# Spectrum stores on GpSimd's queue, a new layout of the attention's inputs, a bias table in DRAM and query parts in two runs, in a one-core encoder kernel

## The chip, the cores and the metric

The kernel runs on one core of a Trainium2 chip, as one program in one launch. The metric is the device time of an execution in microseconds (us). A core has TensorE (PE in the profile, with its weight loads under PEld), VectorE (DVE), ScalarE (ACT), GpSimd (POOL) and SyncE (SP). Each runs its own instruction stream in order, semaphores join the streams, and any of SP, ACT and POOL can issue DMAs from its stream; such an issue stands in the engine's order like any other instruction.

## The reference

One layer of an encoder on 2048 + 256 = 2304 tokens of width 1024, in fp32:

```python
h = rmsnorm(x); q, k, v, u, qm = split(h @ w_in)           # 8 + 2 + 2 heads of 64, 256 channels, 4 heads
y_attn = window attention of q on k, v (|t-s| <= 128, bias -2^-(head+1) * |t-s|, sink logit per head)
y_four = real(fft2(u)) over (positions, channels of a group)
y_mem  = cross attention of qm on k, v of 256 memory tokens
x = x + concat(rmsnorm(y_attn), rmsnorm(y_four), rmsnorm(y_mem)) @ w_out
x = x + square(relu(rmsnorm(x) @ w_ff1)) @ w_ff2
return rmsnorm(x)
```

## The kernel before, in words

**Arithmetic.** An fp32 product is done as three matmuls of a split: `hi` is a copy of a number in the matmul's rounded fp32 type, `lo` the rest. `hi_of` (L103) makes the first on ScalarE, `lo_of` (L106) the second on VectorE. `scaled_split` (L169, L170) does both with a gain, for the output weights: `woh` on ScalarE, then `wol` on VectorE, which needs `woh`. All matmuls go through one helper, L100. `rstd_of` (L133, L134) makes 1/root of a mean square on GpSimd.

**Stages.** First the in-projection. Its groups g = 0 to 8 hold 256 tokens each, with two memory groups between; a group's tokens are normalised, transposed, split and multiplied by the resident `win`. Each group stores k, v and q to DRAM scratch (`Kd`, `Vd`, `Qd`). A part of q is copied from the PSUM tile `pj` in eight pieces of 64 partitions: four by ScalarE (L420, the rounded copy) and four by VectorE (L421, the rest), each VectorE piece after the ScalarE piece that it subtracts. In groups 2 to 6 a side job, `w2_sums`, loads tiles of the second feed-forward weight, subtracts parts of them on GpSimd and stores them to DRAM, through two buffers `big`. In groups 7 and 8 another side job, `fourier`, does the DFT over positions: it combines channels into `X` and `fbig` (L530 on GpSimd among others), loads the DFT matrices `seq` from GpSimd's queue (L445), multiplies (`po`), and `spread` turns a result into rows: copies L482 and L484, squaring L491 (`fjk`), rstd on GpSimd, scaling L493 (`fst`), and a store of 128 KB to `Yd0`, `Yd1` or `Zd` (L495, from ScalarE's queue). `mirror` (L473) copies rows of `Zd` to `Yd0`, in reversed order, in two DMAs, also from ScalarE's queue. The last group's three q stores (L424) go from ScalarE's queue too; those of the groups before go from SyncE's.

Then the attention with the out-projection. Blocks of 128 tokens are loaded in pairs (`load_pair`): keys `kb` (L621) and values `vb` (L634) of up to four blocks, queries `qb` of each block (L632), memory keys and values `km`, `vm` (L646, L648). For the first pair there is also the table of distances `dist` (L624), from which GpSimd makes the table `bias`, eight heads of 128x384 bf16 (L626). Scores `s` are matmuls of `qb` and `kb`; `p` (L661, VectorE) adds the bias and takes the least, L664 (ScalarE) is the exponential; `t` transposes it for the product with `vb`. Fourier rows `y` come back from DRAM (L758). `open_out` loads the eight 128x1024 slices `wos_0` to `wos_7` of the output weights (L813) into three buffers and splits them; the out-projection `op` of a block needs all eight pairs of `woh` and `wol`, and the block's `x` again (`xr`, L825). The feed-forward stage, with its own tilings, takes the rest of the time, from about 870 us on; the change does not touch it.

**What sets the order.** The program text gives what depends on what; a scheduler puts the instructions of each engine in order when the program is built, and that order is fixed. Pools of tiles lie on a left and a right side of the on-chip memory (SBUF). A later pool may lie over an earlier one; each of its tiles then waits for the last users of the tiles beneath it. The attention's pools lie over the in-projection's `fpool` (left): before the change `kb_0` over `wl0`, `vb_0` over the tiles of x, `bias` and `qb_0` over `X` and neighbours, `qb_1`, `km`, `vm` over the small Fourier buffers and `fbig0`, and the buffers of `p`, one of which held `dist`, over `fbig0` and `fbig1`. The output weights (right side) lie over `win`.

Of the kernel before, what the change touches and what calls it, by code (L numbers as in the profile page):

```python
# [12 lines left out]
F32R = mybir.dt.float32r  # L13
BF16 = mybir.dt.bfloat16
AF = mybir.ActivationFunctionType
ALU = mybir.AluOpType
# [4 lines left out]
P = 128  # L21
# [72 lines left out]
def trunk(ctx, tc, x, mem, w_in, w_mem, w_out, w1, w2, gains, g_final, sinks, ident_d, dist_d, cdft_d, seq_d, y):  # L94
# [20 lines left out]
    mhalf = cpool.tile([P, 4], F32, name="mhalf")  # L115
    dve.memset(mhalf, -0.5)

    Qd = dpool.tile([NBLK, P, NQ, P], F32R, name="Qd")
    Kd = dpool.tile([P, 2, 2, T], F32R, name="Kd")
    Vd = dpool.tile([NBLK, P, 2, 2, HD], F32R, name="Vd")  # L120
# [25 lines left out]
    if True:  # L146
# [62 lines left out]
        def w2_sums():  # L209
            ts = {}  # L210
            for j in range(NF // 2 + 1):
                if j < NF // 2:
                    ts[j] = big(f"w2r_{j}")
                    sp.dma_start(ts[j].rearrange("p (k n) c -> p k (n c)", k=2), w2[2 * j:2 * j + 2].rearrange("k p n -> p k n"))
                yield
                if j > 0:
                    b = ts.pop(j - 1)
                    for o, u, v in ((0, 1, 0), (1, 3, 1), (3, 3, 0), (2, 3, 2)):
                        pool.tensor_tensor(out=b[:, o], in0=b[:, u], in1=b[:, v], op=ALU.subtract)
                    pool.dma_start(W2T[j - 1], b)  # L220
                yield

        w2_work = w2_sums()

# [147 lines left out]
        def group(g, side=None):  # L372
# [5 lines left out]
            for mp in (3, 2, 0, 1, 4):  # L378
# [33 lines left out]
                else:  # L412
# [2 lines left out]
                    pv = ps.rearrange("p j (b t) -> p j b t", b=2)  # L415
                    for e in range(2):
                        a = slice(e * HD, (e + 1) * HD)
                        o = slice((1 - e) * HD, (2 - e) * HD)
                        for j in range(2):
                            act.activation(qv[a, e, j], pv[a, j], AF.Copy, scale=-0.125)  # L420
                            dve.scalar_tensor_tensor(out=qv[o, e, j], in0=pv[a, j], scalar=-0.125,  # L421
                                                     in1=qv[a, e, j].bitcast(F32), op0=ALU.mult, op1=ALU.subtract)
                    h0 = {0: 0, 1: 4, 4: 8}[mp]
                    (act if g == 8 else sp).dma_start(  # L424
                        Qd[2 * g:2 * g + 2, :, h0:h0 + 4].rearrange("b p h t -> p b (h t)").bitcast(F32),
                        q.rearrange("p b j e t -> p b (j e t)").bitcast(F32))
                if 2 <= g < 7:
# [38 lines left out]
        def place(ti, r):  # L466
            if ti > 8:
                return Y1[:, ti - 9]
            return Zd[7 - ti] if r else Y0[:, ti]

        def mirror(a):

            act.dma_start(Y0.rearrange("t r c -> r t c")[9 + a:16:2, ::-1], Zd[a:7:2])  # L473


        def spread(ti, po, full):
# [15 lines left out]
            rstd_of(st, 256)  # L492
            act.activation(yr[:, 0:n], yr[:, 0:n], AF.Copy, scale=st)  # L493
            for r in range(n):
                act.dma_start(place(ti, r), yr[:, r])  # L495

        def fourier():
            yield
# [85 lines left out]
        for i, name in enumerate(order):  # L584
            g = int(name[1:])
            if name[0] == "m":
                mem_kv(g, i)
            elif g < 7:
                if g == 3:
                    fe, fab, ffg = f8("fe"), f8("fab"), f8("ffg")  # L590
                group(g)
        for _ in w2_work:
            pass
        side = fourier()
        group(7, side)
        group(8, side)
# [4 lines left out]
    right.close()  # L601
    left.close()
    if True:
        ip = {k: region(left, "left", "in_" + k) for k in ('kk', 'vv', 'bias', 'q', 'mem', 'p')}
        op = region(right, "right", "outproj")
        ps_p = region(right, "right", "ps_p", 1, PSUM)
        inner, banks_ = ExitStack(), ExitStack()
# [6 lines left out]
        def load_pair(b0):  # L614
            r = b0 >= NB0
            first = b0 in (0, NB0)
            last = b0 + 2 in (NB0, NBLK)
            ka, kz = b0 - (not first), b0 + 2 + (not last)
            nk = kz - ka
            kk = ip["kk"].tile([P, 2, 2, 4 * P], F32R, tag="kk", bufs=2, name=f"kb_{b0}")  # L620
            sp.dma_start(kk[:, :, :, 0:nk * P].bitcast(F32), Kd[:, :, :, ka * P:kz * P].bitcast(F32))  # L621
            if b0 == 0:
                dist = ip["p"].tile([P, 1024], BF16, tag="p", bufs=4, name="dist")[:, 0:3 * P]
                sp.dma_start(dist, dist_d)  # L624
                for u in range(NH):
                    pool.tensor_scalar(out=bias[:, u], in0=dist, scalar1=2.0 ** -(u + 1), scalar2=0.0,  # L626
                                       op0=ALU.mult, op1=ALU.add)
            vv = ip["vv"].tile([P, 4, 2, 2, HD], F32R, tag="vv", bufs=2, name=f"vb_{b0}")
            pair = []
            for b in (b0, b0 + 1):  # L630
                q = ip["q"].tile([P, NQ, P], F32R, tag="q", bufs=3, name=f"qb_{b}")
                sp.dma_start(q.bitcast(F32), Qd[b].bitcast(F32))  # L632
                if b == b0:
                    sp.dma_start(vv[:, 0:nk].rearrange("p b v l d -> p b (v l d)").bitcast(F32),  # L634
                                 Vd[ka:kz].rearrange("b p v l d -> p b (v l d)").bitcast(F32))
                lo = max(b - 1, ka)
                hi = min(b + 2, kz)
                stt = bp.tile([P, 40], F32, tag="stats", bufs=4, name=f"stats_{b}")
                pair.append(dict(b=b, r=r, j0=lo - ka, nk=hi - lo, c0=(lo - b + 1) * P, q=q, k=kk, v=vv, st=stt))
            return pair  # L640
# [743 lines left out]
```

## Time and profile before

| | us |
|---|---|
| median of 3 runs (lowest to highest) | 2340.67 (2337.38 to 2342.37) |
| the profiled execution | 2344.84 |
| its span in the trace | 2343.0 |
| TensorE busy in the span | 2229.2 (95%) |
| VectorE, ScalarE, GpSimd busy | 1561.4, 1003.4, 1139.7 |
| last matmul of the in-projection ends | 357.6 |
| first score matmul of the attention | 371.69 |
| first out-projection matmul `op` | 416.70 |

A name in the trace leaves out the number of a buffer (`kb`, `qb`); L621 is line 621 of the kernel. A row of waits says which engine and line waited, for what, how many us in all, how often, and the longest. `<-` after an idle time names what ended it. "issue" is time in which an engine waited for nothing that the profile shows. In a row of DMA issues the last number is the median us from issue to landing.

### The profile page before, as it was taken

To read this page: it belongs to the slowest core of one execution; us is meant where nothing else is said; L and a number is where in the kernel's file an instruction comes from. 1 tells how busy PE (TensorE), PEld (TensorE's weight loads), DVE (VectorE), ACT (ScalarE), POOL (GpSimd) and SP (SyncE) were. 2 spreads that over 40 slices of the span, in tenths; PEclk is the share of its full clock that TensorE was granted. 3 is DMA by queue.
4 is the path that set the end of the run, shared out by engine and by line. 5 is a ranking of instruction groups with operands and counts; after the bars stand their busy time and mean duration, and the time that the engine had idled before them with its cause. 6 is when DMAs were issued, how large, how long until landed. Compare 5 with 4: busy or idle time off the path is not lost.

```text
span 2343.0 us, 35879 instructions
## 1 busy us (share of the span) xinstructions
PE 2229.2 (95%) x12464; PEld 2005.2 (86%) x12464; DVE 1561.4 (67%) x2781; ACT 1003.4 (43%) x2353; POOL 1139.7 (49%) x1023
## 2 busy tenths in 40 slices
PE   7999996999999999999999899999999999999996
PEld 6999995887788878999999788999998889999984
DVE  7333476777677767888888986555557765555567
ACT  6333356766566654444444433222224342222224
POOL 3554031113123035777777685444444765444476
PEclk9999998999999999999999999999999999999998
DMA  8886347445444368766666887555557675555543
GB/s 298 309 296 246 100 136 280 138 148 158 149 145 156 132 238 298 252 222 228 222 229 222 311 262 272 192 191 190 190 191 268 196 258 187 190 189 190 190 163 99
DMA packets 207116, 488.05 MB, mean 208 GB/s; under 512 B 19799, under 2 KB 63319, under 8 KB 204631
## 3 DMA queue, kind: packets, MB, share of 16 engines
q1 hardware_dynamic: 192896, 446.86, 56.2%
q0 software_dynamic: 6848, 29.24, 3.6%
q10 hardware_dynamic: 7191, 9.65, 1.2%
q8 instruction: 99, 1.62, 0.3%
q14 instruction: 82, 0.67, 0.1%
HBM read 341.76 MB, written 144.83 MB: 208 GB/s over the span
## 4 chain that ended last, share of the span: by engine, by line
PE 67%; DVE 8%; DMA 4%; ACT 2%; issue 2%; POOL 1%; SPq 0%; POOLq 0%; ACTq 0%; DVEq 0%
PE y L100 26%; PE op L100 8%; PE pc L100 8%; PE pb L100 8%; PE pa L100 8%; PE pd L100 4%; DMA X2d<-xr 1%; DVE acc L323 1%; PE s L100 1%; PE ot L100 1%; PE t L687 1%; DVE p L661 1%; DMA XTl<-Xn 1%; DVE al L106 1%; PE otm L100 1%
## 5 line engine op out<-in xcount | busy, mean ns | idle before, releaser
L106 POOL TENSOR_TENSOR w2l<-w,w2h 128x512 fp32r<-128x512 f32 x336 | 484.3, 1443 | 494.8 <-ACT w2h L103 490.2
L100 PE MATMUL y<-w2l,ah 128*128 128x512 f32 x966 | 380.9, 395 | 6.4 <-POOL w2l L106 6.4
L100 PE MATMUL y<-w2h,al 128*128 128x512 f32 x966 | 381.9, 396 | 0.0
L100 PE MATMUL y<-w2h,ah 128*128 128x512 f32 x966 | 360.7, 398 | 17.6 <-DVE acc L323 9.0
L103 ACT ACTIVATE ah<-m 128x384 fp32r<-128x384 f32 x240 | 125.8, 524 | 509.5 <-PE y L100 488.0
L106 DVE TENSOR_TENSOR al<-m,ah 128x384 fp32r<-128x384 f32 x240 | 182.9, 763 | 180.2 <-ACT ah L103 167.6
L323 DVE TENSOR_TENSOR acc<-acc,y 128x512 f32<-128x512 f32 x378 | 244.3, 680 | 24.1 <-PE y L100 20.0
L100 PEld LDWEIGHTS y<-w2h,ah 128*128 128x128 f32 x966 | 183.3, 190 | 45.2 <-DVE acc L323 12.1
L100 PE MATMUL pc<-XTh,w1s 128*128 128x384 f32 x768 | 218.8, 340 | 0.8 <-DVE m L323 0.3
L100 PE MATMUL pa<-XTh,w1s 128*128 128x384 f32 x768 | 215.7, 337 | 0.7 <-ACT w1s L103 0.5
L100 PE MATMUL pb<-XTh,w1s 128*128 128x384 f32 x768 | 214.5, 336 | 0.7 <-ACT m L1095 0.7
L103 ACT ACTIVATE w2h<-w 128x512 fp32r<-128x512 f32 x336 | 207.3, 617 | 10.9 <-DMA w1s<-W1D 4.5
L100 PEld LDWEIGHTS y<-w2h,al 128*128 128x128 f32 x966 | 183.3, 190 | 33.1
L100 PEld LDWEIGHTS y<-w2l,ah 128*128 128x128 f32 x966 | 183.3, 190 | 30.4 <-POOL w2l L106 7.8
L100 PE MATMUL pj<-hl_x,winh 128*128 128x256 f32 x720 | 206.1, 288 | 0.7 <-DVE hl_x L106 0.7
L100 PE MATMUL pj<-hh_x,winh 128*128 128x256 f32 x720 | 203.5, 288 | 1.3 <-ACT hh_x L103 1.3
L100 PE MATMUL pj<-hh_x,winl 128*128 128x256 f32 x720 | 204.5, 286 | 0.0
L1068 DVE SCALAR_TENSOR_TENSOR m<-m 128x384 f32<-128x384 f32 x192 | 159.0, 828 | 42.5 <-ACT m L1095 39.0
L100 PEld LDWEIGHTS pc<-XTh,w1s 128*128 128x128 f32 x768 | 142.9, 190 | 10.4 <-DVE m L323 1.4
L100 PEld LDWEIGHTS pb<-XTh,w1s 128*128 128x128 f32 x768 | 141.2, 188 | 8.9 <-ACT m L1095 1.0
L100 PEld LDWEIGHTS pa<-XTh,w1s 128*128 128x128 f32 x768 | 141.6, 188 | 8.3 <-ACT w1s L103 0.8
L100 PEld LDWEIGHTS pj<-hl_x,winh 128*128 128x128 f32 x720 | 139.3, 194 | 1.3 <-DVE hl_x L106 1.2
(243 smaller groups left out, 5181.4 us busy)
## 6 DMA issues: line engine op xcount, KB each, us to landing
w1s<-W1D SPq DMA_DIRECT2D x224, 512.0 KB, 3.5
W1D<-w1s SPq DMA_DIRECT2D x112, 512.0 KB, 3.6
w<-in_w_dram SPq DMA_DIRECT2D x208, 256.0 KB, 3.8
w<-W2T SPq DMA_DIRECT2D x192, 256.0 KB, 3.6
w2r<-in_w_dram SPq DMA_DIRECT2D x16, 1024.0 KB, 7.3
W2T<-w2r POOLq DMA_DIRECT2D x16, 1024.0 KB, 6.2
XTl<-Xn SPq DMA_DIRECT2D x21, 768.0 KB, 7.7
qb<-Qd SPq DMA_DIRECT2D x18, 768.0 KB, 6.3
```

Of the source, the lines that this page charges most:

```text
L100: pe.matmul(out, lhsT, rhs, start=start, stop=stop, skip_group_check=more)
L103: act.activation(out, src, AF.Copy, scale=scale)
L106: (eng or dve).tensor_tensor(out=out, in0=src, in1=hi.bitcast(F32), op=ALU.subtract)
L323: TT(out=o, in0=a, in1=b, op=ALU.add)
L661: dve.tensor_tensor_reduce(out=p[:, 0:n], in0=s[:, 0:n], in1=bias[:, u, c0:c0 + n], scale=1.0, scalar=nsink[:, u:u + 1], op0=ALU.add, op1= ...
L687: pe.transpose(t[:, j], p[:, j * P:(j + 1) * P], ident)
L1068: dve.scalar_tensor_tensor(out=r, in0=r, scalar=0.0, in1=r, op0=ALU.max, op1=ALU.mult)
```

## The change

1. The 18 stores of `spread`, the two of `mirror` and the last group's three q stores are issued from GpSimd's queue in place of ScalarE's.
2. The pools of the attention's inputs are split and put in another order: `kv0` (keys and values of even pairs), `bias`, `q0`, `q1`, `q2`, `mem`, `p`, `kv1`. By address `kb_0` now lies over `wl0`, `vb_0`, `bias` and `qb_0` over the tiles of x, `qb_1` and `qb_2` over `X` and neighbours, `p` over `fv`, and `kb_2`, `vb_2` over `fbig1` and `fbig0`.
3. At the start of group 6, after what is left of `w2_sums`, GpSimd makes the bias table in a `big` buffer and stores it to DRAM (`Bd`); the attention loads it from there (SyncE's queue, after `qb_0`). `dist` and the eight GpSimd steps leave the attention's start.
4. The eight pieces of a part of q are written in two runs, four on ScalarE and then four on VectorE.

```diff
+        def bias_table():
+            bt = big("bias").rearrange("p k c -> p (k c)").bitcast(BF16)
+            dist, bias = bt[:, 0:3 * P], bt[:, 512:512 + NH * 3 * P].rearrange("p (u c) -> p u c", u=NH)
+            pool.dma_start(dist, dist_d)
+            for u in range(NH):
+                pool.tensor_scalar(out=bias[:, u], in0=dist, scalar1=2.0 ** -(u + 1), scalar2=0.0, op0=ALU.mult, op1=ALU.add)
+            pool.dma_start(Bd, bias)
...
                     for e in range(2):
                         a = slice(e * HD, (e + 1) * HD)
+                        for j in range(2):
+                            act.activation(qv[a, e, j], pv[a, j], AF.Copy, scale=-0.125)
+                    for e in range(2):
+                        a = slice(e * HD, (e + 1) * HD)
                         o = slice((1 - e) * HD, (2 - e) * HD)
                         for j in range(2):
-                            act.activation(qv[a, e, j], pv[a, j], AF.Copy, scale=-0.125)
                             dve.scalar_tensor_tensor(out=qv[o, e, j], in0=pv[a, j], scalar=-0.125,
...
-                    (act if g == 8 else sp).dma_start(
+                    (pool if g == 8 else sp).dma_start(
...
-            act.dma_start(Y0.rearrange("t r c -> r t c")[9 + a:16:2, ::-1], Zd[a:7:2])
+            pool.dma_start(Y0.rearrange("t r c -> r t c")[9 + a:16:2, ::-1], Zd[a:7:2])
...
-                act.dma_start(place(ti, r), yr[:, r])
+                pool.dma_start(place(ti, r), yr[:, r])
...
+                if g == 6:
+                    for _ in w2_work:
+                        pass
+                    bias_table()
...
-        ip = {k: region(left, "left", "in_" + k) for k in ('kk', 'vv', 'bias', 'q', 'mem', 'p')}
+        ip = {k: region(left, "left", "in_" + k) for k in ('kv0', 'bias', 'q0', 'q1', 'q2', 'mem', 'p', 'kv1')}
...
-            if b0 == 0:
-                dist = ip["p"].tile([P, 1024], BF16, tag="p", bufs=4, name="dist")[:, 0:3 * P]
-                sp.dma_start(dist, dist_d)
-                for u in range(NH):
-                    pool.tensor_scalar(out=bias[:, u], in0=dist, scalar1=2.0 ** -(u + 1), scalar2=0.0,
-                                       op0=ALU.mult, op1=ALU.add)
...
+                if b == 0:
+                    sp.dma_start(bias, Bd)
```

The order of SyncE's queue from the last v store of the in-projection on, before (numbers in names tell buffers and tiles apart; those behind the last underscore are the build's own):

```order
L369 DMA Vd_68<-vs_8_4125 128x2x256
L621 DMA kb_0_4433<-Kd_67 128x4x384
L624 DMA dist_4435<-in_dist_dram 128x384
L632 DMA qb_0_4446<-Qd_66 128x1536
L634 DMA vb_0_4445<-Vd_68 128x3x256
L632 DMA qb_1_4450<-Qd_66 128x1536
L646 DMA km_0_4453<-Kmd_69 128x2048
L648 DMA vm_0_4455<-Vmd_70 128x1024
L621 DMA kb_2_4602<-Kd_67 128x4x512
L632 DMA qb_2_4605<-Qd_66 128x1536
L634 DMA vb_2_4604<-Vd_68 128x4x256
L813 DMA wos_0_4479<-in_w_out_dram 128x1024
```

And the same place in SyncE's queue of the changed kernel:

```order
L379 DMA Vd_69<-vs_8_4137 128x2x256
L826 DMA wos_0_4488<-in_w_out_dram 128x1024
L826 DMA wos_1_4492<-in_w_out_dram 128x1024
L826 DMA wos_2_4496<-in_w_out_dram 128x1024
L826 DMA wos_3_4500<-in_w_out_dram 128x1024
L826 DMA wos_4_4504<-in_w_out_dram 128x1024
L638 DMA kb_0_4451<-Kd_68 128x4x384
L643 DMA qb_0_4454<-Qd_67 128x1536
L645 DMA bias_4450<-Bd_66 128x3072
L647 DMA vb_0_4453<-Vd_69 128x3x256
L643 DMA qb_1_4459<-Qd_67 128x1536
L659 DMA km_0_4462<-Kmd_70 128x2048
```

Five of the eight loads of output weights have moved ahead of the attention's first loads. They have three buffers, so `wos_3` waits until `wol_0` has read `wos_0`, and `wos_4` until `wol_1` has read `wos_1`. `kb_2` and `vb_2` (not in these rows of the changed kernel) follow later and wait for the stores that empty `fbig1` and `fbig0`.

ScalarE at the end of the in-projection before (`q_8_4` is the last part of q, `fst_9`, `fst_10` the last Fourier tiles, `p_0_0` the first exponential of the attention):

```order
L493 ACTIVATE fbig0_3569<-fbig0_3569,fst_9_4313 128x256
L491 ACTIVATE fjk_10_4325,fst_10_4324<-fbig1_3570 128x256
L495 DMA Yd1_73<-fbig0_3569 128x256
L424 DMA Qd_66<-q_8_1_4255 128x2x512
L493 ACTIVATE fbig1_3570<-fbig1_3570,fst_10_4324 128x256
L420 ACTIVATE q_8_4_4380<-pj_8_4_4331 64x2x128
L495 DMA Yd1_73<-fbig1_3570 128x256
L420 ACTIVATE q_8_4_4380<-pj_8_4_4331 64x2x128 x3
L424 DMA Qd_66<-q_8_4_4380 128x2x512
L664 ACTIVATE p_0_0_4460,stats_0_4449<-p_0_0_4460,stats_0_4449 128x256
```

And of the changed kernel:

```order
L429 ACTIVATE q_8_4_4392<-pj_8_4_4343 64x2x128 x4
L506 ACTIVATE fbig1_3582<-fbig1_3582,fst_3_4210 128x512
L504 ACTIVATE fjk_9_4326,fst_9_4325<-fbig0_3581 128x256
L506 ACTIVATE fbig0_3581<-fbig0_3581,fst_5_4298 128x512
L495 ACTIVATE fbig1_3582<-po_10_4314 128x124
L497 ACTIVATE fbig1_3582<-po_10_4314 128x8
L504 ACTIVATE fjk_10_4337,fst_10_4336<-fbig1_3582 128x256
L506 ACTIVATE fbig0_3581<-fbig0_3581,fst_9_4325 128x256
L506 ACTIVATE fbig1_3582<-fbig1_3582,fst_10_4336 128x256
L170 ACTIVATE woh_0_4486<-wos_0_4488,gain_62 128x1024
L170 ACTIVATE woh_1_4484<-wos_1_4492,gain_62 128x1024
L170 ACTIVATE woh_2_4482<-wos_2_4496,gain_62 128x1024
```

The DMAs have left ScalarE, the last part of q stands ahead of the rest of the Fourier tail, and the first five `woh` follow that tail and stand ahead of `p_0_0`. On VectorE `wol_0` to `wol_4` likewise stand directly ahead of the first `p`, where before they came 55 rows and more after it. On TensorE the last Fourier product `po_10` now stands behind the last matmul of the in-projection.

More of the change, by code (lines that the diff above doesn't have):

```diff
@@ L116, in trunk @@
     dve.memset(mhalf, -0.5)
+    Bd = dpool.tile([P, NH, 3 * P], BF16, name="Bd")
     Qd = dpool.tile([NBLK, P, NQ, P], F32R, name="Qd")
@@ L590, in trunk @@
                     fe, fab, ffg = f8("fe"), f8("fab"), f8("ffg")
+                if g == 6:
+                    for _ in w2_work:
+                        pass
+                    bias_table()
                 group(g)
-        for _ in w2_work:
-            pass
         side = fourier()
@@ L619, in load_pair @@
             nk = kz - ka
-            kk = ip["kk"].tile([P, 2, 2, 4 * P], F32R, tag="kk", bufs=2, name=f"kb_{b0}")
+            kv = ip[f"kv{b0 // 2 % 2}"]
+            kk = kv.tile([P, 2, 2, 4 * P], F32R, tag="kk", bufs=1, name=f"kb_{b0}")
             sp.dma_start(kk[:, :, :, 0:nk * P].bitcast(F32), Kd[:, :, :, ka * P:kz * P].bitcast(F32))
-            if b0 == 0:
-                dist = ip["p"].tile([P, 1024], BF16, tag="p", bufs=4, name="dist")[:, 0:3 * P]
-                sp.dma_start(dist, dist_d)
-                for u in range(NH):
-                    pool.tensor_scalar(out=bias[:, u], in0=dist, scalar1=2.0 ** -(u + 1), scalar2=0.0,
-                                       op0=ALU.mult, op1=ALU.add)
-            vv = ip["vv"].tile([P, 4, 2, 2, HD], F32R, tag="vv", bufs=2, name=f"vb_{b0}")
+            vv = kv.tile([P, 4, 2, 2, HD], F32R, tag="vv", bufs=1, name=f"vb_{b0}")
             pair = []
             for b in (b0, b0 + 1):
-                q = ip["q"].tile([P, NQ, P], F32R, tag="q", bufs=3, name=f"qb_{b}")
+                q = ip[f"q{b % 3}"].tile([P, NQ, P], F32R, tag="q", bufs=1, name=f"qb_{b}")
                 sp.dma_start(q.bitcast(F32), Qd[b].bitcast(F32))
+                if b == 0:
+                    sp.dma_start(bias, Bd)
                 if b == b0:
```

## The prediction

> **What bounds the kernel now.** I read the windows first. They split the span into the end of the in-projection, the pause before the attention, the attention's ramp and the steady part (columns: length, then busy time per engine).
>
> ```profile
> 357.60:371.70 14.10, 0.01 (x1) 0.04 (x1) 1.69 (x4) 2.02 (x5) 3.53 (x8) 0.68 0.74 252
> 371.70:416.70 45.00, 37.97 (x203) 29.83 (x204) 38.99 (x108) 39.70 (x112) 5.59 (x8) 0.91 0.79 295
> 416.70:440.00 23.30, 22.57 (x139) 19.36 (x138) 18.24 (x50) 16.27 (x48) 1.61 (x4) 1.00 0.38 127
> 440.00:870.00 430.00, 412.88 (x2358) 348.05 (x2356) 303.76 (x814) 269.22 (x805) 99.95 (x155) 1.00 0.47 156
> ```
>
> TensorE is the bound nearly everywhere (412.88 of 430 us in the steady attention), so this change can win or lose only where TensorE stands: 14.1 us before the attention, 45.00 − 37.97 = 7.0 us in the ramp, and small stalls in the in-projection. Second view: the waits from 340 to 375 us, for what those pauses wait for.
>
> ```profile
> PE s L100 <- DMA qb<-Qd: 14.1, 1, 14.1
> POOL bias L626 <- DMA dist<-in_dist_dram: 10.3, 1, 10.3
> DVE p L661 <- POOL bias L626: 9.2, 1, 9.2
> PE po L100 <- ACT fjk L491: 1.5, 1, 1.5
> ```
>
> Third: SyncE's queue in time order (start, duration, what), its waits, and the chain, which names what released it.
>
> ```profile
> 353.98 0.57 SPq L621 DMA_DIRECT2D kb<-Kd  x1
> 364.81 0.35 SPq L624 DMA_DIRECT2D dist<-in_dist_dram  x1
> 365.21 0.54 SPq L632 DMA_DIRECT2D qb<-Qd  x1
> ...
> 367.98 0.66 SPq L621 DMA_DIRECT2D kb<-Kd  x1
> ```
> ```profile
> SPq L624 <- DMA Yd<-fbig: 9.7, 1, 9.7
> ```
> ```profile
> 356.63 8.02 DMA Yd<-fbig
> ...
> 366.33 6.70 DMA qb<-Qd
> ...
> 398.27 8.43 DMA wos<-in_w_out_dram
> 406.72 1.16 ACT woh L169
> ...
> 416.70 2.32 PE op L100 x10
> ```
>
> The `dist` load goes into a tile laid over the Fourier buffer `fbig0`, waits for its last stores, and holds the first `qb` behind it in the in-order queue. Call T the end of the in-projection on TensorE, 357.6. The first `qb` is issued at T+7.6, the first scores start at T+14.1. Later the chain runs through the third batch of output weights `wos` and their splits into the first out-projection matmul at 416.7.
>
> **The change part by part.** *Layout, stores on GpSimd, bias from DRAM (judged together, since all act on the pause).* The `dist` load and the wait for `fbig` are gone. By the diff alone the first inputs, now over tiles free early, would land under TensorE's work. But the new order of SyncE's queue puts `wos_0` to `wos_4` ahead of `kb_0`: `wos_3` reuses the buffer of `wos_0` and waits for `wol_0`, `wos_4` for `wol_1`. These splits stand behind the Fourier tail on ScalarE. I time that tail from the old one (ScalarE's timeline; the last row is the last piece of q before the attention).
>
> ```profile
> 359.48 0.51 ACT L493 ACTIVATE fbig<-fbig,fst 128x256 f32<-128x256 f32 x1 [2.48 <-issue]
> ...
> 362.61 0.38 ACT L420 ACTIVATE q<-pj 64x256 fp32r<-64x256 f32 x1 [0.49 <-DVE q L421]
> ```
> ```profile
> L134 POOL TENSOR_TENSOR fst<-fst,mhalf 128x1 f32<-128x1 f32 x11 | 7.3, 666 | 0.7
> ```
> ```profile
> L169 ACT ACTIVATE woh<-wos,gain x8: 1152/1154/1166, 389.3 to 410.3; 128x1024 fp32r<-128x1024 f32 x8
> L170 DVE SCALAR_TENSOR_TENSOR wol<-wos,gain,woh x8: 1274/1278/1285, 391.2 to 412.8; 128x1024 fp32r<-128x1024 f32 x8
> ```
>
> After T ScalarE now has four pieces of q (4 × 0.38 = 1.5), four scalings (4 × 0.51 = 2.0), two squarings and two small copies (about 1.7 by the same rows, an estimate) and one GpSimd step between the last squaring and scaling (0.67): 5.9, with a hand-over to VectorE about T+6.7. Then woh_0 (1.15) and wol_0 (1.28) end at T+9.1, wol_1 at T+10.4. Three issues at SyncE's 0.4 to 0.6 us each put kb_0 at T+10.8, qb_0 at T+11.4 and the bias (128×3072 bf16, 768 KB) at T+12.0. The landing times:
>
> ```profile
> qb<-Qd SPq DMA_DIRECT2D x5, 768.0 KB, 7.3
> kb<-Kd SPq DMA_DIRECT2D x2, 1024.0 KB, 9.8
> wos<-in_w_out_dram SPq DMA_DIRECT2D x8, 512.0 KB, 7.7
> Yd<-fbig ACTq DMA_DIRECT2D x6, 128.0 KB, 6.8
> ```
>
> A bias of 768 KB takes 7.3 like qb, so it lands at T+19.3. The first `p`, which stands behind wol_4 on VectorE, would by wos_4 (issued T+10.4, 7.7, plus 1.15 and 1.28) start no later than T+20.5. I take T+19.6. Before, `p` started when the last of eight bias steps was done:
>
> ```profile
> L626 POOL TENSOR_SCALAR bias<-dist x8: 513/514/519, 368.2 to 372.0; 128x384 bf16<-128x384 bf16 x8
> ```
>
> 372.0 + 0.5 is T+15.0 (with the hand-over). So the pause **grows by 4.6 us**. Bounds: +2.5 if wos and bias land in 5 us instead of 7.3 to 7.7, +8 if the bias shares the queues with vb, qb_1 and km and takes kb's 9.8 and woh_0 also waits for its load (T+7.7).
>
> *The ramp.* Five of eight woh and wol now lie in that pause. ScalarE loses 5 × 1.15 = 5.8 us and VectorE 5 × 1.28 = 6.4 us of 39.70 and 38.99 busy in the 45 us, in which TensorE's own work is 37.97. One more row of the woh tile shows what else goes:
>
> ```profile
>   DMA wos<-in_w_out_dram: 1.9, 1
> ```
>
> I take VectorE's 6.4: **−6.4 us**. It cannot pass TensorE's idle 7.0, and if only the chain's wait for wos (1.9) and two splits (2.4) shorten, it is −4.
>
> *The two runs of q.* Before, ScalarE and VectorE took turns on each of the eight pieces and waited for each other (row of the q tile over the in-projection: idle us and times).
>
> ```profile
>   ACT q L420: 51.3, 45
>   DVE q L421: 31.5, 42
> ```
>
> With four ScalarE pieces first and then four on VectorE the turn-taking falls away; VectorE gets free sooner for the splits of x and of the memory tokens. Where TensorE waits there:
>
> ```profile
> PE tp_m L182 <- DVE hl_m L106: 3.8, 2, 2.0
> PE tp_x L182 <- DVE x L166: 2.5, 2, 1.4
> PE tp_x L182 <- DVE hl_x L106: 2.2, 1, 2.2
> PE tp_m L182 <- DVE m L166: 1.6, 2, 0.9
> ```
>
> That is 10.1 us, of which the first rows come before there is any q; 31.5 + 51.3 us of mutual waiting do not lie on TensorE's path, so only part returns. I take a fifth, −2.0, and the 1.5 us stall of po at 350, which waits for ScalarE while that is held by issuing stores (2.48 us of "issue" in the row above), goes with the stores: T moves by **−3.5** (from 0, if every stall stays or the reordered tail adds one, to −5).
>
> *Stores on GpSimd.* 11 + 7 stores, two mirrors and three Qd stores leave ScalarE. GpSimd already issues loads in this stretch:
>
> ```profile
> L445 POOL DMA_DIRECT2D seq<-in_seq_dram x9 | 5.3, 592 | 5.2 <-PE po L100 5.1
> ```
>
> At 0.59 us each the 23 cost 13.6 us on an engine that waits for others in this stretch (10.3 for `dist`, 5.1 for po). Queued behind a waiting store are seq loads and the rstd steps of later blocks; the last is a mirror, waiting for its Zd stores, then two Yd1 stores, on which kb_2 waits. Nominally: last Zd issue T+4, landing T+10.8 (6.8), mirror and two stores to T+12.6, landing T+19.4, kb_2 landing 9.8 later, T+29.2. Its first scores came at
>
> ```profile
> 396.34 1.16 PE L100 MATMUL s<-kb,qb 128*128 128x384 f32 x4
> ```
>
> (the second two of the four), thus at T+39 and now, with the pause, at T+43: hidden with 14 us to spare. Cost nothing; +12 if that cover is gone (rival B). The Trainium skill's page "SBUF — State Buffer", section "A bandwidth-pool intuition that's wrong (but worth ruling out)", speaks against the move: a DMA issued by GpSimd takes about 620 ns alone and about 3100 ns beside a copy on VectorE, because GpSimd cannot write descriptors while VectorE holds the shared port. The row's 592 ns, with VectorE busy beside it, agrees with the first figure; by the second figure the 23 stores would take some 71 us (estimate from that page).
>
> *The bias table in group 6* puts one load, eight steps of 0.51 (4.1 us) and a store on GpSimd where it waits for data; nothing queued behind is due soon. Nothing; +1 if the rstd steps of group 7 slip.
>
> **Sum**: −3.5 + 4.6 − 6.4 = −5.3 us. The profiled execution took 2344.84 us (span 2343.0 and 1.84 around it); it becomes 2339.5. That run lies 4.2 above the median of the three, 2340.67, so the median becomes 2335.4. A measurement of this kernel can tell about 0.2%, 4.7 us, from no change: the forecast lies just beyond that border.
>
> **The rivals.** *A, no change*: the turn-taking of q was hidden, as TensorE's full windows say, and the ramp stays bound by the chains of p, pth and y instead of the splits (−4). With both, T by the stall of po alone: −1.5 + 4.6 − 4 = −0.9, 2339.8 us. For it speaks that 82.8 us of waits in q cost TensorE at most 10.1; against it that VectorE and ScalarE are 87 and 88% busy in the ramp.
>
> *B, slower*: GpSimd's queue drains late. In its order 15 issues stand from the Qd store of q_8_0 to the last Yd1 store. If VectorE's work stretches each to over 2.5 us, they last 15 × 2.5 = 37 us; begun at T−8 they end at T+29, land at T+36, and kb_2 lands at T+46 (9.8) against T+43. That is the point from which B decides. At 3.1 each the last lands at T+45, kb_2 at T+55: +12 on −5.3, 2347.4 us. For it: no row of before shows GpSimd issuing stores of this kind in this stretch; against it: 592 ns for the loads. The Trainium skill's page named above gives those 3100 ns, in the same section; no run here has shown them.
>
> *C, the change does what its layout says*: kb_0, qb_0 and the bias land while TensorE still works; of the 14.1 us some 2 stay for the hand-over from q, and the ramp keeps its splits: −3.5 − 12 = −15.5, 2325.2 us. Against it: the queue's order, with kb_0 behind wos_4.
>
> **How the numbers follow.** Forecast 0.53, A 0.30, B 0.11, C 0.06. Predicted 2335.4. The three terms' best ends together (−5, +2.5, −7) give −9.5, 2331.2, and a run differs by another us or so: low 2330, which leaves out most of C. Their worst ends (0, +8, −4) give +4, 2344.7; they seldom meet, so high 2344, which leaves out B. Faster by over 0.2% means below 2336.0: four fifths of the forecast's case, whose better end is the wider (0.42), and C, 0.48 together. Slower by over 0.2% means above 2345.3: B, 0.11. Within: the rest of the forecast's case (0.11) and A, 0.41.
>
> **What would show it.** Right: kb is issued after two wol, about T+11; the first p at T+19 to T+21; five woh before it; op L100 starts 43 us or less after the first s instead of 45; T at 353 to 356 us. Wrong: kb issued before T; TensorE waiting for kb_2; seq or store issues on GpSimd over 2 us; T later than 357.6; the gaps after the ramp growing.

## The result and the profile after

The changed kernel takes 2353.40 us in the median of four runs (2351.34 to 2355.05), the kernel before 2340.04 (2337.38 to 2342.37): a ratio of 1.0059 with a 95% interval of 1.0044 to 1.0074, 13.4 us slower where 5.3 us faster was forecast. The profiled execution spans 2353.3 us against 2343.0, 10.3 us more. It lies 1.7 us above the median of its runs, that of the kernel before 4.8 us, so a stretch of one profile can be off by some us.

I cut both traces at four places that both have: T (here the start of the last in-projection matmul `pj`; the prediction's 357.6 is its end), the first `p` on VectorE, the first feed-forward matmul `pa`, and the first read of the scratch `W1D` by SyncE, some 450 us into the feed-forward stage.

| us | before | after | difference |
|---|---|---|---|
| T | 357.3 | 351.5 | −5.8 |
| T to first `p` | 15.3 | 30.1 | +14.8 |
| first `p` to first `pa` | 492.0 | 485.9 | −6.1 |
| first `pa` to first read of `W1D` | 444.8 | 452.5 | +7.7 |
| from there to the end | 1033.6 | 1033.3 | −0.3 |
| span | 2343.0 | 2353.3 | +10.3 |

Two places lose, the pause and a stage that the change does not write to. First the pause, in the windows (columns as before):

```profile
351.80:381.60 29.80, 2.70 (x10) 2.28 (x10) 8.74 (x14) 10.48 (x20) 6.78 (x12) 0.56 0.73 274
381.60:413.00 31.40, 28.09 (x166) 22.85 (x167) 29.11 (x92) 29.86 (x94) 1.48 (x4) 0.93 0.86 316
```

TensorE works 2.70 of 29.80 us. The chain through that stretch names each step:

```profile
343.73 11.44 DMA Yd<-fbig
355.26 0.64 ACT q L429 x2
...
359.88 0.57 POOL Yd L508
...
362.97 1.05 ACT woh L170
...
365.24 1.29 DVE wol L171
366.97 0.57 SPq L638
...
369.12 12.29 DMA bias<-Bd
```

A spectrum store issued by GpSimd at 343.73 lands 11.44 us later. `spread` writes its rows into four buffers in turn, and ScalarE's next write into that one (L497) waits for the landing; everything behind it on ScalarE stands still, the last part of q among it:

```profile
ACT fbig L497 <- DMA Yd<-fbig: 6.0, 1, 6.0
PE po L100 <- ACT fjk L504: 6.1, 1, 6.1
POOL Yd L508 <- ACT fbig L506: 7.8, 1, 7.8
DVE p L674 <- DMA bias<-Bd: 3.7, 1, 3.7
```

Then come `woh_0`, `wol_0`, `wol_1`, and only then SyncE's first attention load, as the forecast had it, but at T+15.5 in place of T+10.8:

```profile
342.83 24.09 SPq L826 DMA_DIRECT2D wos<-in_w_out_dram  x5
366.97 0.57 SPq L638 DMA_DIRECT2D kb<-Kd  x1
```

The loads, issued close together, then land late. The issues from 343 to 382 us, with the median landing in the last column:

```profile
Yd<-fbig POOLq DMA_DIRECT2D x6, 128.0 KB, 10.4
bias<-Bd SPq DMA_DIRECT2D x1, 768.0 KB, 12.3
```

The second place is the start of the feed-forward stage. TensorE's timeline there, with the idle time ahead in brackets, and a window:

```profile
895.57 0.69 PE L100 MATMUL pa<-XTh,w1s 128*128 128x384 f32 x1 [4.71 <-ACT w1s L103]
```
```profile
891.80:905.40 13.60, 9.42 (x35) 8.19 (x36) 5.61 (x9) 4.17 (x8) 3.82 (x3) 0.75 1.01 375
```

TensorE waits 4.71 us for a split `w1s` on ScalarE. Before, the same wait was 0.45 us, at full clock:

```profile
888.40 0.44 PE L100 MATMUL pa<-XTh,w1s 128*128 128x384 f32 x1 [0.45 <-ACT w1s L103]
```
```profile
884.70:898.30 13.60, 11.92 (x62) 10.55 (x61) 7.26 (x13) 5.37 (x10) 4.13 (x3) 1.00 0.99 335
```

The granted clock of 0.75 in the window of the changed kernel is half clock for 6.8 of the 13.6 us. Finer windows show where:

```profile
894.75:895.57 0.82, 0.00 (x0) 0.00 (x1) 0.54 (x1) 0.77 (x2) 0.82 (x1) 0.51 0.85 300
895.57:901.58 6.01, 5.60 (x14) 4.51 (x15) 5.07 (x9) 1.04 (x2) 0.40 (x1) 0.50 1.05 410
```

The first 0.8 us of it still lie in the stall. In the other 6.0 us TensorE works 5.60 us at half rate, which costs 2.8 us. The longer wait (4.3) and the half clock (2.8) make 7.1 of the 7.7; the rest is not placed. The scheduler, which orders the whole program, had put ScalarE's work there in another order (the built order, which both traces show):

```
before: w1s_0_0_3  w1s_0_1_1  w2h_0_0_1_0  w2h_0_0_1_1  ...
after:  w1s_0_0_3  w2h_0_0_1_0  w2h_0_0_1_1  ...  w1s_0_1_1  ...
```

The split of the next tile now stands behind two splits of the second weight, whose loads come later.

### The profile page after: what moved, and what is told of

The parts are those of the page before. It is cut to its first block, busy times and chain, and to the rows that moved or that the text cites. A ratio compares the mean times of both kernels' runs of the same rounds, so it can differ in the third digit from the quotient of the medians.

```text
span 2353.3 us, 35931 instructions
## 1 busy us (share of the span) xinstructions
PE 2228.6 (95%) x12464; PEld 2006.0 (85%) x12464; DVE 1561.5 (66%) x2781; ACT 998.5 (42%) x2353; POOL 1151.2 (49%) x1048
## 4 chain that ended last, share of the span: by engine, by line
PE 74%; DVE 8%; DMA 8%; POOL 3%; ACT 3%; issue 3%; SPq 0%; POOLq 0%; ACTq 0%; DVEq 0%
PE y L100 26%; PE op L100 8%; PE pb L100 8%; PE pc L100 8%; PE pa L100 8%; PE pj L100 6%; PE pd L100 4%; DMA w2r<-in_w_dram 3%; DMA X2d<-xr 2%; POOL w2r L220 1%; DVE acc L333 1%; PE s L100 1%; PE ot L100 1%; PE t L700 1%; DMA XTl<-Xn 1%
## 5 line engine op out<-in xcount | busy, mean ns | idle before, releaser
L100 PEld LDWEIGHTS y<-w2h,ah 128*128 128x128 f32 x966 | 183.5, 191 | 42.8 <-DVE acc L333 10.1
L100 PEld LDWEIGHTS pc<-XTh,w1s 128*128 128x128 f32 x768 | 142.9, 190 | 10.4 <-DVE m L333 2.3
```

The costliest lines, as they stand in the source:

```text
L100: pe.matmul(out, lhsT, rhs, start=start, stop=stop, skip_group_check=more)
```

## The experiments

Theories at the outset: **W**, the pause grew because the attention's first loads stand behind five loads of output weights; **G**, because GpSimd's stores land late; **F**, the rest of the loss is the order at the feed-forward start; **S** (found at e3), the first `p` is held by a tile laid over the last spectrum stores. Totals and ratios are against the kernel before on the same chip. Places of single profiled executions scatter: the five kernels with the in-projection of the changed kernel (it, e1, e3, e5, e13) have T from 346.2 to 353.8. So I compare stretches, and totals by the medians. In the columns: T, T to first `p`, first `p` to `pa`, `pa` to `W1D` read, all us.

| run | T | to `p` | to `pa` | to `W1D` | median | ratio (95%) |
|---|---|---|---|---|---|---|
| e1 weights requested later | 353.3 | 30.8 | 486.5 | 446.2 | 2345.56 | 1.0020 (1.0010 to 1.0031) |
| e2 bias from DRAM alone | 356.1 | 14.7 | 491.4 | 452.9 | 2347.63 | 1.0031 (1.0021 to 1.0040) |
| e3 weights behind the bias | 351.8 | 25.8 | 491.4 | 451.9 | 2353.98 | 1.0060 (1.0045 to 1.0075) |
| e4 q in turns | 358.3 | 18.8 | 488.2 | 448.3 | 2354.23 | 1.0057 (1.0042 to 1.0073) |
| e5 as e3, y first | 346.2 | 10.9 | 502.0 | 453.2 | 2348.64 | 1.0035 (1.0022 to 1.0048) |
| e6 as e8, y first | 347.8 | 16.4 | 492.0 | 445.7 | 2338.84 | 0.9993 (0.9984 to 1.0003) |
| e7 stores on GpSimd alone | 358.2 | 20.4 | 487.0 | 444.8 | 2345.84 | 1.0027 (1.0018 to 1.0036) |
| e8 stores back on ScalarE | 350.6 | 19.7 | 489.9 | 444.6 | 2339.44 | 0.9996 (0.9985 to 1.0007) |
| e9 two runs of q alone | 351.4 | 21.3 | 487.4 | 444.7 | 2338.30 | 0.9986 (0.9976 to 0.9995) |
| e10 18 stores on GpSimd alone | 354.9 | 13.3 | 493.6 | 451.9 | 2345.81 | 1.0025 (1.0009 to 1.0040) |
| e11 layout alone | 357.3 | 11.9 | 489.7 | 443.5 | 2338.84 | 0.9995 (0.9985 to 1.0004) |
| e12 mixed version | 351.6 | 17.0 | 496.8 | 445.0 | 2342.94 | 1.0013 (1.0003 to 1.0022) |
| e13 bias loaded before q | 353.8 | 31.8 | 483.4 | 444.6 | 2347.33 | 1.0026 (1.0014 to 1.0038) |
| e14 layout, y first | 357.3 | 8.5 | 498.4 | 447.5 | 2340.89 | 0.9991 (0.9978 to 1.0005) |
| e15 layout, y first, q in runs | 352.0 | 17.4 | 490.4 | 446.6 | 2337.19 | 0.9985 (0.9975 to 0.9994) |

**e1**, the changed kernel, output weights requested later:

```diff
-            if n == 0:
+            if n == 12:
                 open_out()
```

> The changed kernel with the output weights requested later in the program text (after the thirteenth attention unit instead of the first). In the built order the start of the attention stays as in the changed kernel (five wos ahead of kb_0, five woh ahead of the first exponential), but ScalarE's order at the start of the feed-forward stage is again that of the kernel before. Theory F (about 7 us of the loss is that order: a w1s split behind two w2h splits, TensorE waiting 4.7 us and then 6.8 us more at half clock): first p stays at about 381, the 4.7 us wait of pa for w1s goes, total 2344 to 2348. Rival G (the loss is GpSimd's stores and the pause alone, the feed-forward part an after-effect of it): no gain, 2351 to 2356.

As F has it: the pause stays (30.8), the feed-forward start comes out as before (446.2), and the total falls to 2345.56.

**e2**, the kernel before with part 3 alone (`bias_table`, its load, no `dist`).

> The kernel before with the bias table from DRAM alone. The built order at the attention's start is that of before without dist; at the feed-forward start it is that of the changed kernel. Theory F: the first p comes 5 to 9 us earlier (about 365), part of it lost again in the ramp, and the feed-forward start loses about 7: total 2337 to 2344, and the trace shows pa waiting some 4 to 5 us for w1s. Rival (no effect of the order at the feed-forward start): 2331 to 2336 and no such wait.

F again: `pa` waits 5.0 us for `w1s`, the stretch takes 452.9. But the pause hardly shrank, though SyncE issued the first qb at 353.88 and scores began at 360.4: `p` came at 370.8. Something other than inputs held it. The total, 2347.63, lies above the expected range.

**e3**, the changed kernel with the first weights tied behind the bias:

```diff
                 s = op.tile([P, D], F32, tag="xr", bufs=3, name=f"wos_{k}")
+                if k < 3:
+                    pool.tensor_copy(out=s[:, 0:8], in_=bias[:, 0, 0:8])
                 sp.dma_start(s, w_out[k * P:(k + 1) * P, :])
```

> The changed kernel in which the first three wos tiles are touched by GpSimd with a value of the bias before they are loaded (the load overwrites it), so that they must follow the bias: SyncE's order becomes kb_0, qb_0, bias first, wos after y_0. The feed-forward order stays the changed kernel's. Theory W (the pause grew because kb, qb and the bias stand behind wos_4): kb is issued before T, the first p comes at 360 to 366, before the 372.6 of the kernel before; the five pairs of splits go back into the ramp, and the total is 2339 to 2347. Rival G (GpSimd's stores land late and hold ScalarE): the first p stays later than 372, the total 2350 or more.

W, as it was put, fell. SyncE issues kb before T, and `p` comes at 377.6, where 360 to 366 was expected; that is 4.0 us earlier than in the changed kernel. SyncE's row, and the waits from 343 to 400 us:

```profile
343.11 0.57 SPq L638 DMA_DIRECT2D kb<-Kd  x1
```
```profile
PE s L100 <- DVE stats L674: 17.4, 2, 16.2
DVE p L674 <- DMA Yd<-fbig: 15.7, 1, 15.7
```

The first `p` also writes its row minima into `stats_0`. That tile, the lowest of the attention's small tiles on the right side, lies over `fbig0`, so VectorE waits there for the last stores out of `fbig0`, whatever the inputs do. In the changed kernel itself the last two stores were issued here:

```profile
364.72 1.11 POOL L508 DMA_DIRECT2D Yd<-fbig  x2
```

They landed at 375.2 and 375.7, the bias at 381.4. So in that kernel both hold `p`: the late stores beyond the 372.6 of the kernel before, and then the bias, which is late with the other loads.

**e4**, the changed kernel with the eight pieces of q in turns, as before.

> The changed kernel with the eight pieces of q in turns as before (stores on GpSimd, layout and DRAM bias stay). The built order has only wos_0 and wos_1 ahead of kb_0, which wait for no split. Theory W: kb, qb and bias are issued when TensorE ends or before, the first p comes at 362 to 368, total 2335 to 2343 (its feed-forward order is a third one, unknown by plus or minus 7). Rival G: GpSimd's stores are the same, so the pause stays at 19 us or more and the total at 2350.

The built order had only two weight loads ahead of kb, and kb, the first qb and the bias were issued by 344, but:

```profile
DVE p L669 <- DMA Yd<-fbig: 10.9, 1, 10.9
```

The same wait as in e3, and `p` at 377.1: once the loads are early, the order of SyncE's queue no longer decides. The total, 2354.23, is no better than that of the changed kernel, although T to `p` is 11.3 us shorter; T is later by 6.8.

**e5**, e3 with `y` of block 0 taken from the pool ahead of `stats`, so that `y`, written later, lies over `fbig0`:

```diff
+                y0 = bp.tile([P, D], F32, tag="y", bufs=3, name="y_0") if b == 0 else None
                 stt = bp.tile([P, 40], F32, tag="stats", bufs=4, name=f"stats_{b}")
...
-            B["y"] = bp.tile([P, D], F32, tag="y", bufs=3, name=f"y_{b}")
+            B["y"] = B["y0"] if b == 0 else bp.tile([P, D], F32, tag="y", bufs=3, name=f"y_{b}")
```

> The kernel of run e3 (weights behind the bias) with one more edit: the y tile of block 0 is taken from the pool of mixed tiles before the stats tile, so that y and no longer stats lies over fbig0. In e3 the inputs had landed at 361, but the first p, which writes stats, waited to 377.6 for the last spectrum stores out of fbig0. Theory S (that tile under stats is what holds the first p): the first p comes at 361 to 366, 12 to 16 us earlier, and y, written some 11 us later, takes over the wait; total 4 to 12 us below e3's 2354, 2342 to 2350. Rival W2 (the Fourier tail on ScalarE and VectorE holds p as well): the first p at 370 or later and the total within 3 us of e3.

S holds: T to `p` falls from 25.8 to 10.9 us, and what is left of the wait has moved to `y`:

```profile
DVE y L736 <- DMA Yd<-fbig: 2.3, 1, 2.3
...
DVE p L675 <- DMA bias<-Bd: 0.9, 1, 0.9
```

Of those 14.9 us the attention gives back 10.6 (502.0 against 491.4). All eight pairs of splits come after the first `p` in both runs. What did not move is SyncE's `kb_2`, which lies over `fbig1` and `fbig0` and waits for the same stores, with the weights behind it in the queue. In e3 and in e5:

```profile
377.89 0.55 SPq L638 DMA_DIRECT2D kb<-Kd  x1
```
```profile
373.16 0.55 SPq L638 DMA_DIRECT2D kb<-Kd  x1
```

That is T+26.1 and T+27.0. From T to the first `op` it is 59.2 us in e3 and 53.9 in e5, and the total falls by 5.3.

**e6**, the changed kernel with the stores on ScalarE (as e8) and the edit of e5.

> The changed kernel with the stores back on ScalarE's queue and y in place of stats over fbig0. In the built order only wos_0 stands ahead of kb_0, and ScalarE's order at the feed-forward start is that of the kernel before. Theory S with theory F: the first p comes at 358 to 366 and pa does not wait for w1s; of the 8 to 14 us won at the pause half or more stays: total 2326 to 2335, below the kernel before. Rival (the ramp gives it all back, since ScalarE and VectorE bound it): 2337 to 2342.

The first `p` came at 364.2 as expected, 8.4 us earlier than before, but the total did not: 2338.84, not to be told from before. The span of the profile is 7.3 us shorter, of which the medians show 0.7: the profile of e6 lies 1.4 us below its median, that of the kernel before 4.8 above. T to `p` is still 16.4; run e8 shows what holds ScalarE there.

**e7**, the kernel before with part 1 alone, and **e10**, of part 1 only the 18 stores of `spread` (mirrors and q stores back on ScalarE).

> The kernel before with the stores on GpSimd's queue alone. Feed-forward order as before. Theory G (GpSimd's stores land later, and dist, in a tile over fbig0, and stats wait for the last of them): SyncE issues dist at 374 to 382 in place of 364.8, the first p comes 8 to 16 us later than 372.6, part of it returned by two early pairs of splits: total 2344 to 2352. Rival (the queue does not matter): the first p at 369 to 375, total 2336 to 2341.

> The kernel before with only the 18 stores of spread on GpSimd's queue; the mirrors and the last q stores stay on ScalarE's. (Feed-forward order of the changed kernel, some 7 us.) In run e7 the last two stores stood behind a mirror and a q store of 512 KB each on GpSimd's queue, were issued at 363.6 to 364.7 and landed at 372.5. Theory M (what is queued ahead of them on that queue makes them late): dist is issued at 362 to 368 and the first p comes at 369 to 374. Rival (a store issued by GpSimd is slow by itself): dist at 371 or later, first p at 377 or later. Total by theory M 2344 to 2349, by the rival 2350 to 2355.

They tell what is late about GpSimd's stores. In e7, SyncE's `dist` and GpSimd's end of the tail:

```profile
372.55 0.33 SPq L624 DMA_DIRECT2D dist<-in_dist_dram  x1
```
```profile
361.64 1.19 POOL L473 DMA_DIRECT2D Yd<-Zd  x1 [1.36 <-DMA Zd<-fbig]
362.84 0.75 POOL L424 DMA_DIRECT2D Qd<-q  x1
363.58 1.13 POOL L495 DMA_DIRECT2D Yd<-fbig  x2
```

And in e10:

```profile
358.24 0.35 SPq L624 DMA_DIRECT2D dist<-in_dist_dram  x1
```
```profile
353.51 0.54 POOL L495 DMA_DIRECT2D Yd<-fbig  x1
...
359.37 0.61 POOL L495 DMA_DIRECT2D Yd<-fbig  x1 [3.12 <-ACT fbig L493]
```

In e7 the last two stores of 128 KB stand on GpSimd's queue behind a mirror, which waits for the `Zd` stores, and a q store, 512 KB each. `dist` waits for the first of the two, out of `fbig0`, which landed at 372.3, and gets through at 372.55, 7.7 us later than before. In e10, without the mirror and the q store on that queue, the store that `dist` waits for was issued at 353.51 and landed at 358.0, `dist` got through at 358.24, and T to `p` is 13.3. So a store from GpSimd is not slow by itself; what stands ahead of it on its queue made it late. Of the 14.3 us between the two landings 10.1 lie before the issue and 4.2 between issue and landing; in e7 GpSimd had stood 6.5 us for a q store (at 355.2) and 1.4 for the mirror.

In e7 `dist` and `p` came somewhat before the ranges of theory G, in e10 before those of theory M; both totals came as these theories had them. e7 loses 6.0 us at the pause and nothing in the feed-forward stage, e10 nothing at the pause and 7.1 there. In e10 that accounts for the total. In e7 it agrees with the medians (6.3), while the profile's span is only 1.4 us longer, since its stretch from `p` to `pa` is 5.0 shorter.

**e8**, the changed kernel with part 1 undone.

> The changed kernel with the stores back on ScalarE's queue alone. Feed-forward order as before, one wos ahead of kb_0. Theory G with S: the stores land earlier, but stats still lies over fbig0, so the first p waits for the last store and comes at 366 to 371: total 2334 to 2340. Rival W (only the order of SyncE's queue mattered): kb, qb and bias have landed by 362 and the first p comes at 358 to 364: total 2327 to 2334, equal to run e6.

As G with S had it, `p` comes at 370.3. The whole loss is gone (0.9996): here, without the stores on GpSimd, neither the late pause nor the other feed-forward order comes up. That order does not hang on those stores, though: e2 has it without them, and e7, with all of them, does not. And nothing is won, although T is at 350.6. ScalarE's timeline:

```profile
357.16 0.65 ACTq L485 DMA_DIRECT2D Yd<-Zd  x1
357.85 6.10 ACTq L507 DMA_DIRECT2D Yd<-fbig  x1
363.98 0.77 ACTq L436 DMA_DIRECT2D Qd<-q  x1
364.80 0.42 ACT L503 ACTIVATE fjk<-fbig 128x256 bf16<-128x256 f32 x1 [9.71 <-DMA bias<-Bd]
```

A store on ScalarE's queue takes 6.10 us to issue, and ScalarE, in order, stands idle for 9.71 us. The trace puts the end of that down to the landing of the bias, but the mirror, the long issue and the q store fill the stretch from 357.16 to 364.75 by themselves. In all eight kernels with these stores on ScalarE the long issue is that of the store behind the second mirror. It takes 2.26 and 2.10 us where of the attention's inputs only kb is out (before, e9), 4.74 to 4.83 with `dist` and qb out (e11, e14, e15), and 6.10 to 6.61 with qb and the bias out (e2, e6, e8). That early loads hold up the stores behind which the first `p` waits agrees with these numbers; it is not shown, since no run has the store without the mirror ahead of it.

**e9** and **e11**, the two runs of q alone, and the layout alone.

> The kernel before with the two runs of q alone. Feed-forward order as before; one wos ahead of kb_0; dist still waits for the stores out of fbig0. The runs with the two runs of q so far ended the in-projection at 346 to 353, those without at 356 to 358. Theory Q (the two runs shorten the in-projection by some 5 to 7 us and dist's wait keeps the rest of the pause): T at 347 to 353, first p at 365 to 370, total 2332 to 2337. Rival (the pause takes it back, since the tail is ScalarE's stores and not TensorE): first p at 370 to 374, total 2338 to 2342.

> The kernel before with the new layout of the pools alone. The built order is that of before, at the feed-forward start too. dist goes into the first tile of p, which lies over fv and is free early, so it no longer waits for fbig0; but stats does lie over the last stores. Theory S: qb issued by 356, the first s at 361 to 364, the first p at 368 to 372, total 2336 to 2340, not to be told from before. Rival (the inputs' layout is what held the first p): the first p at 362 to 366, total 2331 to 2336.

In e9 T moves to 351.4, but `dist` still waits for the stores (issued at 366.80) and `p` comes at 372.7, where it was: of the 6 us at T some 1.4 stay in the total. The ramp with one split moved out of it takes 4.6 less, which the profile of one execution shows and the medians do not. e11 came out as S has it, no difference in the total.

**e12**, a version put together (18 stores on GpSimd, layout, bias, two runs of q, y first, weights requested later).

> A version put together from the readings: the changed kernel with only the 18 spread stores on GpSimd, y in place of stats over fbig0, and the output weights requested after the thirteenth unit. In its built order wos_0 to wos_2, which wait for no split, stand ahead of kb_0, and the feed-forward start has the order of the kernel before. By theories Q, S, M and F together: T at 346 to 353, first p at 358 to 364, no wait of pa for w1s, total 2327 to 2334. Rival (the ramp returns what the pause gives, as in runs e5 and e6): 2336 to 2340.

A miss: the three `wos` took SyncE 13.0 us to issue, kb came at 358.4, the first `p` at 368.6 and T to `p` was 17.0; the total lies above the rival's range too. SyncE waited 11.6 us there, by the trace for a mirror on ScalarE's queue; why stays open.

**e13**, the changed kernel, one DMA moved by one place:

```diff
+            if b0 == 0:
+                sp.dma_start(bias, Bd)
             pair = []
             for b in (b0, b0 + 1):
                 ...
-                if b == 0:
-                    sp.dma_start(bias, Bd)
```

> The changed kernel with one DMA moved by one place: the bias is loaded before qb_0 and not after it. The built order keeps wos_0 to wos_4 ahead of kb_0 and all stores on GpSimd, but the feed-forward start comes out in the order of the kernel before. Theory F, without the other edits of run e1: from the first pa to the first read of W1D 444 to 447 us in place of 452.5, no wait of pa for w1s, the pause as in the changed kernel (first p about 30 us after T), total 2344 to 2348. Rival (the loss in the feed-forward part follows from the late start): 451 us or more there, total 2351 to 2355.

The pause is the changed kernel's (31.8 us), all stores are on GpSimd, and the feed-forward start has the order of before. TensorE's timeline and the window there:

```profile
891.90 0.44 PE L100 MATMUL pa<-XTh,w1s 128*128 128x384 f32 x1 [0.34 <-ACT w1s L103]
```
```profile
892.00:905.40 13.40, 12.32 (x63) 10.92 (x64) 9.00 (x15) 4.96 (x9) 6.99 (x6) 1.00 1.00 364
```

The wait is 0.34 us, the clock 1.00, the stretch 444.6, and the ratio falls from 1.0059 to 1.0026. F is shown: the loss is the order, and no result of the late start, for the first `pa` comes at 869.0, later than in the changed kernel (867.5). In the table the five kernels with the changed kernel's order take 451.9 to 453.2 us there (after, e2, e3, e5, e10), those with the order of before 443.5 to 447.5, and e4, with a third order, 448.3.

**e14** and **e15**, the kernel before with the layout and y first, then with the two runs of q as well.

> The kernel before with the new layout of the pools and y in place of stats over the last spectrum buffer; stores on ScalarE, dist and the eight bias steps as before, order of every engine as before. In run e11 the first p waited 4.5 us for the stores under stats. Theory S: the first p comes at 362 to 366 (once ScalarE and VectorE are through with q), and a part of the 4.5 us stays: total 2334 to 2338, faster than before by 0.1 to 0.25%. Rival (the ramp, bound by ScalarE and VectorE, returns it): 2338 to 2341.

> Run e14 with the two runs of q as well (one wos ahead of kb_0, feed-forward order as before). Theories Q and S add: T at 346 to 352, the first p at 357 to 363, total 2329 to 2335. Rival (the end of the pause is set by ScalarE's queue of stores and not by T): the first p as in e14, total 2334 to 2340.

In e14 T to `p` is 8.5 us, the shortest of all, and the attention returns nearly all of it (498.4); its weights are requested at 371.96, before at 372.72. In e15 ScalarE is held again:

```profile
364.43 0.42 ACT L494 ACTIVATE fjk<-fbig 128x256 bf16<-128x256 f32 x1 [8.01 <-DMA qb<-Qd]
```

The first `p` comes at 369.4. Both totals went with the rivals. Still e15, at 2337.19 against 2340.97, is the one version here, with e9, whose interval lies below 1 (0.9975 to 0.9994): 0.15% or 3.8 us faster than before, where 6 to 12 were expected.

## Why the prediction was wrong

Between the forecast of −5.3 and the 10.3 of the two profiles lie 15.6 us: 10.2 in the pause, 7.7 in the feed-forward stage, −2.3 in T.

- *What bounds the kernel, and where the change can act.* Right for the pause and the ramp. Wrong in its end: the sum stopped at the first out-projection and had no term for the feed-forward stage. That step is worth +7.7 us of the 10.3 between the two profiles, shown by e1 and e13. The scheduler orders the whole program, and a change at the attention's start moved a `w1s` split behind two `w2h` 500 us later. No single part does it: the new order came with part 3 alone (e2) and with the 18 stores alone (e10), and not with part 1 (e7), the two runs (e9) or the layout alone (e11).
- *The pause, +4.6.* It grew by 14.8, from T; the first `p` came 9.0 us later. The order was read rightly: kb did come after `wol_1`. Two sizes in the sum failed and make up the miss. The Fourier tail was taken to run through, with the hand-over at T+6.7: it stood 6.0 us for a store that landed after 11.44 in place of 6.8, `woh_0` began at T+11.4, and the bias was issued at T+17.6 in place of T+12.0. And the bias was to land in 7.3, at most 9.8: it took 12.3. That is 5.6 + 5.0 us. Besides, the step took the inputs for all that the first `p` waits for. The prediction had the last `Yd1` stores in its working, landing at T+19.4, but let only kb_2 wait for them. They landed at T+24, and `stats` over `fbig0` would have held `p` until then anyway, as e3 and e4 show. Of the 9.0 us the stores alone bring 6.0 (e7), and early loads alone take back 4.0 (e3).
- *Stores on GpSimd at no cost.* Right on the issue, wrong on the queue. The row of the changed kernel:

```profile
L508 POOL DMA_DIRECT2D Yd<-fbig x11: 539/566/636, 321.0 to 365.3; - x11
```

They issue in 566 ns, near the 592 of the row used. The figure of about 3100 ns beside a VectorE `tensor_copy`, from the Trainium skill's page "SBUF — State Buffer", section "A bandwidth-pool intuition that's wrong (but worth ruling out)", does not appear in any of these issues. VectorE's steps beside them are tensor_tensor and scalar_tensor_tensor, so no run here tests it for a copy. The cost was what stands ahead on the queue: part 1 alone loses 6 us (e7), and without mirrors and q stores nothing at the pause (e10).
- *The ramp, −6.4.* Measured −6.1 from `p` to `pa`: the direction is right, the size is not shown. TensorE idles 7.0 us in the 45.0 us of the ramp's window before, and 3.3 (31.40 − 28.09) in the 31.4 us of that of the changed kernel. And e9 and e7, with one and two pairs of splits moved, show −4.6 and −5.0 in the same stretch, which their medians do not. The end of the ramp was misread: 416.7 is where the chain enters a run of `op` matmuls. The first `op` starts at 407.0 before and at 411.7 after, 35.3 and 32.0 us after the first score; before, that is ahead of the last split (412.8), so `op` begins without all eight pairs.
- *T, −3.5.* Measured −5.8. Of the kernels with the two runs of q T is 346.2 to 353.8, of those without 354.9 to 358.3. So the direction was right. But the last Fourier product `po_10`, 1.5 us of TensorE, now stands behind T, which is a part of the −5.8. And the stall of `po`, which was to go with the stores, grew from 1.5 to 6.1 us: `po_10` ends at 359.4, later than all of the in-projection before (357.6). In e9, with the stores on ScalarE, it ends at 353.2, and yet little of that reaches the end while stores set the end of the pause.
- *Rival B*, slower through GpSimd's late queue, had the right sign and engine and the wrong mechanism: not slow issues and not kb_2, which nobody waited for, but late landings that held ScalarE and the first `p`. *Rival C* was rightly unlikely for this order. Its loads alone would not have done either: with kb issued before T (e3) the pause stayed 25.8 us, and only with `y` in place of `stats` (e5) did it fall to 10.9.

What stays open: why a store on ScalarE's queue takes 5 to 6 us to issue once the loads are out (e8, e15), and what part the mirror ahead of it has in that; why SyncE waited in e12; and which 3.1 us of the 13.4 between the medians the two profiles do not show.

## What to carry to other kernels

When a wait is to be removed, list everything that the first instruction behind it touches, its small outputs too: here a `stats` tile of 160 bytes a partition kept a wait that a new layout of all inputs was made to remove. Then ask what waits next for the same thing: with that tile out of the way `p` came 20.5 us earlier (e5 against e3), and the weights, behind a load that waits for the same stores, only 4.7. Before stores are moved to another in-order queue, ask which transfers, and which waits for other results, will stand ahead of the one that somebody waits for. And where a scheduler orders the whole program, compare the order of the later stages as well: a few instructions swapped 500 us away cost nearly as much as the pause itself.

## What the runs showed of the hardware

- One stall of TensorE of 4.71 us brought 6.8 us at half clock (0.75 in a window of 13.6 us), 0.8 of them still in the stall; with a stall of 0.34 us at the same place the clock was 1.00. The stall and the half clock cost 4.71 + 2.8 us, 1.6 times the stall alone. The Trainium skill's page "TensorE: Matmul & The Clock Gate", section "What's actually happening", has the half rate after idle windows of about 3.4 us. The stall of 4.71 us agrees. But stalls of 2.87 and 2.88 us of TensorE at the start of this stage (`xp`, in the kernel before and in the changed one) and one of 2.78 us for `w1s` (e10) brought 6.8 us at half clock too, so standing still for 3.4 us was not needed here. In all 17 profiles the stretches at half clock between the first `pa` and the read of `W1D` last 3.4 or 6.8 us.
- A 128 KB store landed in a median of 6.8 us in the tail before and in 10.4 after, with loads of weights and q stores under way; the 768 KB loads of qb landed in 7.3 before, the one of the bias in 12.3 after. GpSimd's issues of these stores took 539 to 636 ns all the same.
